# Other filler tiles: the streamed and held operands of the split matmuls start at other bytes of a 256-byte line

## The chip, the core and the metric

One NeuronCore of one Trainium2 chip runs the whole program in one launch. The metric is device time in microseconds (us), the median of several runs. The engines are named as in the profile: PE (TensorE, matmul) and PEld (its weight load), DVE (VectorE), ACT (ScalarE), POOL (GpSimd), SP (SyncE, which issues the DMAs).

## The reference

Two networks run one after the other on 256 tokens of width 1024, in float32, each of two layers. All heavy work is matrix products `x @ w` with x of 256 rows:

```python
# first block, per layer (sizes: 256 x 1024 in, FFN hidden 2816)
u = rms_norm(h, g_mix_pre)
gq, gk, gv, gg, ra_f, ra_b, aq, ak, av, gate_a, gate_b = split(u @ w_in)
...   # gated linear attention, grouped-query attention with axial rope
mixed = sigmoid(gate_a) * branch_a + sigmoid(gate_b) * branch_b
h = h + rms_norm(mixed @ w_out, g_mix_post)
gate, up = split(rms_norm(h, g_ffn_pre) @ w_ffn_in, 2)
h = h + rms_norm((silu(gate) * up) @ w_ffn_out, g_ffn_post)
h = h + rms_norm(sigmoid(h @ w_ple_gate) * (p_i @ w_ple_proj), g_ple_post)
# second block, per layer
x = x + 0.5 * swiglu_ffn(rms_norm(x, ffn1_norm), ffn1_w_in, ffn1_w_out)
...   # recurrent branch (conv, rg_lru) and forgetting attention, merged
x = x + merged @ w_o
x = x + 0.5 * swiglu_ffn(rms_norm(x, ffn2_norm), ffn2_w_in, ffn2_w_out)
x = x + sigmoid(rms_norm(x, ple_norm) @ ple_w_gate + ple_b_gate) * (p_i @ ple_w_proj)
```

## The kernel before

Every big product is made of three matmuls in the format fp32r: a float32 operand is split into a high part and a low part (`hi`, `lo` for a weight; names that end in `h` and `l` for an activation: `xTh`/`xTl`, `hh`/`hl`, `oh`/`ol`, `yh`/`yl`, `mh`/`ml`, `xrh`/`xrl`, `px`), and high x high, high x low and low x high are added up in PSUM. Weights come in tiles of 512 KB from HBM (`raw`), ACT makes `hi` (L250), DVE makes `lo` (L251).

There are two ways to multiply, and they use the operands the other way round:

- `gemm_fm` (L288 to L290): the weight block of 128 columns is **held** in the array (stationary, loaded by a weight load), the activation of 256 columns is **streamed** through it. All of the input projections by features, both FFN inputs, and all products of the second block but three.
- `gemm_tm` (L315 to L317): the activation block of 128 columns is held, the weight of 512 columns is streamed. In the first block it makes w_aq, w_akv, w_gv, w_gg (held: `xT`), w_out (held: `mh`, `ml`), w_ffn_out (held: `hh`, `hl`), w_ple_gate (held: `xr`) and the small w_ple_proj (held: `px`); in the second block w_v, w_q, w_k (held: `xT`).

In both, matmuls follow each other with a new weight load for each; the load for the next one goes on while this one streams. Beside these, small float32 matmuls serve the attentions and the transposes, and L831 is one more fp32r matmul whose streamed operand (`ra`) and held one (`up`) both lie in the mixer's pool.

SBUF is given out by tile pools, one behind the other: constants, `wraw` (raw weights), `whl` (`hi`, `lo`), `act` (`xT`, `R`), `small`, then the temporaries (`t`, `sq`, `px`, ...) and the pool of the stage (mixer or FFN). A filler is a dead tile at the start of a pool (`Net.phase`): nothing reads or writes it, it only moves what lies behind it in this and the later pools. The fillers decide at which byte of a 256-byte line a tile starts. All the blocks inside a tile start at multiples of 512 bytes from it, so all of them have the start byte of the tile.

The order of the instructions is set by a scheduler when the program is built.

Of the kernel before, what the change touches and what calls it, by code (L numbers as in the profile page):

```python
# [11 lines left out]
F32 = mybir.dt.float32  # L12
# [6 lines left out]
P = 128  # L19
# [20 lines left out]
HOLD_B = 4  # L40
LAG = 3

X_PHASE = 64
POOL_PHASE = 32


class Norm:
# [3 lines left out]
    def __init__(self, net, g, tag="xT"):  # L51
        self.net, self.g = net, g
        self.xs = net.pair(net.act, tag)
        self.r = [None, None]
        self.R = net.act.tile([P, S], F32, tag="R", name=net.name("R"), bufs=2)
        self.ssq = [net.small.tile([P, 2], F32, tag="nssq", name=net.name("nssq")) for _ in range(2)]
# [124 lines left out]
class Net:  # L181
    def __init__(self, ctx, tc, a, raw_bufs=4, w_bufs=5, acc_bufs=3):
        self.tc = tc
        self.nc = tc.nc
        self.a = a
        pool = lambda name, bufs, **kw: ctx.enter_context(tc.tile_pool(name=name, bufs=bufs, **kw))
        psum = bass.MemoryType.PSUM
        self.const = pool("const", 1)
        self.wraw = pool("wraw", raw_bufs)
        self.whl = pool("whl", w_bufs)  # L190
        self.act = pool("act", 1)
        self.small = pool("small", 4)
        self.ps = pool("ps", acc_bufs, space=psum)
        self.pt = pool("pt", 2, space=psum)
        self.pm = pool("pm", 2, space=psum)
        self.pg = pool("pg", 1, space=psum)
        self.n = 0
        self.phase(self.act, X_PHASE)
        self.phase(self.small, X_PHASE)


        self.hold = self.held = None
        self.fetched = []
        nc = self.nc
        self.ident = self.const.tile([P, P], F32, name="ident")
        self.h = self.const.tile([P, 2, D], F32, name="h")
        self.expo = self.const.tile([P, 16], F32, name="expo")
        nc.vector.memset(self.expo, -0.5)
        self.ones = self.const.tile([P, P], F32, name="ones")
        nc.vector.memset(self.ones, 1.0)  # L210

    def phase(self, pool, n):

        pool.tile([P, n // 4], F32, tag="phase", name=self.name("phase"), bufs=1)

    def temporaries(self, ctx, bufs):
        self.tmp = ctx.enter_context(self.tc.tile_pool(name=self.name("tmp"), bufs=1))
# [300 lines left out]
def layer_a(net, i, nrm, following):  # L518
    nc, a, tc = net.nc, net.a, net.tc
    with ExitStack() as mx:  # L520
        nrm, px = mixer_a(net, i, mx, nrm)
    with tc.tile_pool(name=net.name("ffn"), bufs=1) as fp:
        net.phase(fp, POOL_PHASE)
        g_post = net.gain(a["g_ffn_post"][i])
        e = ple_proj(net, px, a["w_ple_proj"][i])
        raw = Raw(net, fp)
        net.ffn(nrm, a["w_ffn_in"][i], a["w_ffn_out"][i], net.post_norm(g_post, raw, fp, HOLD_FFN), fp)
        g_post = net.gain(a["g_ple_post"][i])
        nrm = following()
        px = ple_input(net, a["pT_2"][0]) if i + 1 == DEPTH else None  # L530

        def gated(tt, hf, acc):
            cs = slice(hf * 512, (hf + 1) * 512)
            t = net.t()
            nc.scalar.activation(t, acc, AF.Sigmoid)
            nc.vector.tensor_tensor(t, t, e[:, tt, cs], ALU.mult)
            return t

        net.gemm_tm(raw.xs, a["w_ple_gate"][i], net.post_norm(g_post, nrm, fp, HOLD_PLE if i + 1 < DEPTH else HOLD_LAST, gated), lag=LAG)
    return nrm, px  # L540


def ple_input(net, pT):
    with net.urgent(SPLIT_PRIO, 200):
        raw = net.t()
        net.nc.sync.dma_start(out=raw, in_=pT)
        px = (net.t((P, 2, S), F32R, "px"), net.t((P, 2, S), F32R, "px"))
        net.split_fm(raw, *px, 0)
    return px


def ple_proj(net, px, w):
    nc = net.nc
    e = net.t((P, 2, D), tag="e")
    net.gemm_tm(px, w, lambda tt, hf, acc: nc.scalar.copy(e[:, tt, hf * 512:(hf + 1) * 512], acc))
    return e
# [347 lines left out]
def layer_b(net, i, nrm, px, hT, following):  # L904
# [12 lines left out]
    with ExitStack() as cx:  # L917
        ms = mixer_b(net, i, cx, after)
        px = ple_input(net, a["pT_2"][i])
        nrm = NormT(net, hT, col(2))  # L920
        net.gemm_fm(ms, a["w_o"][i], net.add_scaled(hT, 1.0, nrm.blocks), tail=True)
# [20 lines left out]
def mixer_b(net, i, cx, nrm):  # L942
    nc, a, tc = net.nc, net.a, net.tc
    p1 = cx.enter_context(tc.tile_pool(name=net.name("mx"), bufs=1))
    net.phase(p1, POOL_PHASE)
    big = lambda tag, dt=F32: p1.tile([P, KB, S], dt, tag=tag, name=net.name(tag))
    fl = lambda t: t.rearrange("p a b -> p (a b)")
    xs, rs = nrm.xs, nrm.r
# [143 lines left out]
def _build(tc, a, out):  # L1092
    with ExitStack() as ctx:
        net = Net(ctx, tc, a)
        nc = tc.nc
        with ExitStack() as part:
            net.temporaries(part, T_BUFS_A)
            net.split = SPLIT_A
            nrm = lambda pool: first_norm(net, pool)
            nxt = [lambda: Norm(net, net.gain(a["g_mix_pre"][1])), lambda: Norm(net, net.gain(a["ffn1_norm_2"][0]))]  # L1100
            for i in range(DEPTH):
                nrm, px = layer_a(net, i, nrm, nxt[i])

        hp = ctx.enter_context(tc.tile_pool(name="hT", bufs=1))
        net.hp = hp
        net.temporaries(ctx, T_BUFS_B)
        net.split = SPLIT_B
        hT = hp.tile([P, KB, S], F32, name="hT")
        for tt in range(2):
            for hf in range(2):  # L1110
                ps = net.pt.tile([P, 4, P], F32, tag="pt", name=net.name("pt"))
                for j in range(4):
                    kb = hf * 4 + j
                    nc.tensor.transpose(ps[:, j], net.h[:, tt, kb * P:(kb + 1) * P], net.ident)
                nc.scalar.copy(hT[:, hf * 4:hf * 4 + 4, tt * P:(tt + 1) * P], ps)
        gc = hp.tile([P, 16], F32, name="gc")
        nc.sync.dma_start(out=gc, in_=a["gains_last"])
        nxt = [lambda: NormT(net, hT, gc[:, 0:8]), lambda: NormT(net, hT, gc[:, 8:16], out)]
        for i in range(DEPTH):
            nrm, px = layer_b(net, i, nrm, px, hT, nxt[i])  # L1120
# [140 lines left out]
```

## Time and profile before

| | us |
|---|---|
| median of 3 runs (2343.48 to 2346.03) | 2344.41 |
| the profiled execution | 2343.55 |
| its span, first to last instruction | 2341.8 |

The profile is of one execution; its own time is its span and 1.75 us around it. In a timeline the columns are: start in us, duration in us, engine, line, operation, tile written<-tiles read, size, and count. The durations of matmuls overlap (each is printed until its last result is out), so the pace of PE is read from the starts: the time from one start to the next is called a step here.

### The profile page before, as it was taken

Reading aid. Unit: us, or ns where it says so; the run is one execution under the profiler, and the core shown is the slowest. Engines: PE = TensorE matmul, PEld = TensorE weight load, DVE = VectorE, ACT = ScalarE, POOL = GpSimd, SP = SyncE. Lnnn points to the kernel's source line nnn. Section 1 sums busy time; section 2 is a strip of 40 time slices with the busy share of each in tenths; the row PEclk is TensorE's granted clock in tenths of the full one; section 3 lists DMA queues with packets and bytes.
Section 4 is the critical chain, followed back from the end, with each engine's and each line's share of the span. In section 5 each row is a group of like instructions: output and inputs, shape, how many; then the busy total and the mean of one; then the engine's idle time right before and its main releaser. Section 6 shows DMA issues by size and latency. Waiting matters only on the chain.

```text
span 2341.8 us, 42188 instructions
## 1 busy us (share of the span) xinstructions
PE 2291.4 (98%) x16892; PEld 2168.4 (93%) x16892; DVE 1600.6 (68%) x2133; ACT 1335.3 (57%) x2105; POOL 440.3 (19%) x443
## 2 busy tenths in 40 slices
PE   7999999998999999999999999999999999999997
PEld 6899899777899998799999899999999998999997
DVE  7876766477867765766586867665765677766655
ACT  6875554467764644554457765444644457755444
POOL 5222211064302110211001302110111103112101
PEclk9999999999999999999999999999999999999999
DMA  7445566554455666555665545666566655556662
GB/s 250 147 153 160 179 203 186 178 164 148 145 162 173 204 189 185 171 168 187 187 183 184 158 150 185 185 193 187 174 188 184 187 186 166 152 168 191 189 184 96
DMA packets 117102, 411.53 MB, mean 176 GB/s; under 512 B 14114, under 2 KB 16546, under 8 KB 116906
## 3 DMA queue, kind: packets, MB, share of 16 engines
q1 hardware_dynamic: 116906, 408.84, 56.2%
q8 instruction: 133, 2.18, 0.4%
q14 instruction: 63, 0.52, 0.1%
HBM read 407.74 MB, written 1.05 MB: 175 GB/s over the span
## 4 chain that ended last, share of the span: by engine, by line
PE 89%; DVE 4%; POOL 2%; issue 2%; ACT 1%; DMA 1%; SPq 0%; DVEq 0%; POOLq 0%; ACTq 0%
PE acc L290 22%; PE acc L289 22%; PE acc L288 22%; PE acc L315 6%; PE acc L316 6%; PE acc L317 6%; DVE lo L251 2%; PE sc L582 1%; PE po L593 1%; PE gs L890 1%; ACT hi L250 1%; POOL t L713 1%; POOL tab L689 0%; PE sc L606 0%; POOL hg L75 0%
## 5 line engine op out<-in xcount | busy, mean ns | idle before, releaser
L251 DVE TENSOR_TENSOR lo<-raw,hi 128x512 fp32r<-128x512 f32 (+1 forms) x1062 | 983.2, 952 | 439.5 <-ACT hi L250 437.4
L250 ACT ACTIVATE hi<-raw 128x512 fp32r<-128x512 f32 (+1 forms) x1062 | 824.3, 808 | 761.4 <-PE acc L289 396.1
L288 PE MATMUL acc<-xTh,hi 128*128 128x256 f32 x3296 | 924.3, 281 | 10.3 <-ACT t L1060 7.2
L289 PE MATMUL acc<-xTl,hi 128*128 128x256 f32 x3296 | 927.3, 282 | 0.7 <-DVE xTl L130 0.5
L290 PE MATMUL acc<-xTh,lo 128*128 128x256 f32 x3296 | 926.4, 281 | 0.0
L288 PEld LDWEIGHTS acc<-xTh,hi 128*128 128x128 f32 x3296 | 620.1, 188 | 12.5 <-ACT t L1060 7.7
L289 PEld LDWEIGHTS acc<-xTl,hi 128*128 128x128 f32 x3296 | 622.6, 189 | 2.6 <-DVE xTl L130 1.5
L290 PEld LDWEIGHTS acc<-xTh,lo 128*128 128x128 f32 x3296 | 621.3, 189 | 0.4
L396 POOL TENSOR_TENSOR t<-t,R 128x512 f32<-128x512 f32 x66 | 105.0, 1590 | 612.5 <-ACT t L394 612.5
L290 PE MATMUL acc<-hh,lo 128*128 128x256 f32 x704 | 197.1, 280 | 0.0
L288 PE MATMUL acc<-hh,hi 128*128 128x256 f32 x704 | 196.4, 279 | 0.0
L289 PE MATMUL acc<-hl,hi 128*128 128x256 f32 x704 | 196.4, 279 | 0.0
L315 PE MATMUL acc<-hi,xTh 128*128 128x512 f32 x416 | 165.7, 404 | 5.9 <-ACT hi L250 5.9
L316 PE MATMUL acc<-lo,xTh 128*128 128x512 f32 x416 | 167.4, 402 | 2.1 <-DVE lo L251 2.0
L317 PE MATMUL acc<-hi,xTl 128*128 128x512 f32 x416 | 166.4, 401 | 0.1
L289 PEld LDWEIGHTS acc<-hl,hi 128*128 128x128 f32 x704 | 132.4, 188 | 0.0
L290 PEld LDWEIGHTS acc<-hh,lo 128*128 128x128 f32 x704 | 132.1, 188 | 0.0
L288 PEld LDWEIGHTS acc<-hh,hi 128*128 128x128 f32 x704 | 131.6, 187 | 0.0
L315 PEld LDWEIGHTS acc<-hi,xTh 128*128 128x128 f32 x416 | 78.9, 190 | 23.4 <-ACT hi L250 6.0
L316 PEld LDWEIGHTS acc<-lo,xTh 128*128 128x128 f32 x416 | 79.1, 190 | 21.0 <-DVE lo L251 3.8
L317 PEld LDWEIGHTS acc<-hi,xTl 128*128 128x128 f32 x416 | 78.9, 190 | 18.7 <-DVE xTl L351 0.8
L379 DVE TENSOR_TENSOR t<-acc,R 128x512 f32<-128x512 f32 (+1 forms) x84 | 56.8, 676 | 44.1 <-PE acc L290 44.1
(321 smaller groups left out, 3236.5 us busy)
## 6 DMA issues: line engine op xcount, KB each, us to landing
raw<-ffn_w_in SPq DMA_DIRECT2D x176, 512.0 KB, 3.7
raw<-w_ffn_in SPq DMA_DIRECT2D x88, 512.0 KB, 4.3
raw<-ffn_w_out SPq DMA_DIRECT2D x88, 512.0 KB, 3.6
raw<-w_ffn_out SPq DMA_DIRECT2D x44, 512.0 KB, 4.1
raw<-w_gate SPq DMA_DIRECT2D x32, 512.0 KB, 3.6
raw<-w_gab SPq DMA_DIRECT2D x32, 512.0 KB, 3.7
raw<-w_gqk SPq DMA_DIRECT2D x16, 512.0 KB, 4.0
raw<-w_gv SPq DMA_DIRECT2D x16, 512.0 KB, 3.2
```

Source lines behind the costliest of these rows:

```text
L250: nc.scalar.activation(hi[:, cs], raw[:, cs], AF.Copy)
L251: nc.vector.tensor_tensor(lo[:, cs], raw[:, cs], hi.bitcast(F32)[:, cs], ALU.subtract)
L288: nc.tensor.matmul(o, lhsT=hi[:, cs], rhs=xh[:, kb], start=kb == 0, stop=False)
L289: nc.tensor.matmul(o, lhsT=hi[:, cs], rhs=xl[:, kb], start=False, stop=False)
L290: nc.tensor.matmul(o, lhsT=lo[:, cs], rhs=xh[:, kb], start=False, stop=kb == nkb - 1)
L315: nc.tensor.matmul(o, lhsT=xh[:, kb, ts], rhs=hi[:, cs], start=kb == 0, stop=False)
L316: nc.tensor.matmul(o, lhsT=xh[:, kb, ts], rhs=lo[:, cs], start=False, stop=False)
L317: nc.tensor.matmul(o, lhsT=xl[:, kb, ts], rhs=hi[:, cs], start=False, stop=kb == 2 * n - 1)
L379: self.nc.vector.tensor_tensor(v(out), v(acc), r, ALU.mult)
L396: nc.gpsimd.tensor_tensor(tb, tb, nrm.R.unsqueeze(1).to_broadcast([P, 2, S]), ALU.mult)
L582: nc.tensor.matmul(sc[:, j], lhsT=q_t[:, hp * 2 + j, tt * P:(tt + 1) * P], rhs=k_t[:, hp // 2], start=True, stop=True)
L593: nc.tensor.matmul(out[:, j], lhsT=v(jt, hp // 2), rhs=p_t[:, jt], start=jt == 0, stop=jt == 1)
```

## The change

The fillers get other sizes, and the pools of the first block's FFN and of the second block's mixer get different ones. Nothing else is changed. The built programs have the same instructions in the same order on every engine, with the same waits (16,610 on PE, 2,135 on DVE, 1,987 on ACT, 448 on POOL, 812 on SP); only SBUF addresses differ.

```diff
-X_PHASE = 64
-POOL_PHASE = 32
+ACT_PHASE = 192
+SMALL_PHASE = 64
+FFN_A_PHASE = 96
+MIX_B_PHASE = 32
...
-        self.phase(self.act, X_PHASE)
-        self.phase(self.small, X_PHASE)
+        self.phase(self.act, ACT_PHASE)
+        self.phase(self.small, SMALL_PHASE)
...
     def phase(self, pool, n):
-        pool.tile([P, n // 4], F32, tag="phase", name=self.name("phase"), bufs=1)
+        if n:
+            pool.tile([P, n // 4], F32, tag="phase", name=self.name("phase"), bufs=1)
...
 def layer_a(net, i, nrm, following):
...
-        net.phase(fp, POOL_PHASE)
+        net.phase(fp, FFN_A_PHASE)
...
 def mixer_b(net, i, cx, nrm):
...
-    net.phase(p1, POOL_PHASE)
+    net.phase(p1, MIX_B_PHASE)
```

Start bytes within a 256-byte line, read from the addresses of the two built programs:

| tiles | before | after |
|---|---|---|
| `raw`, `hi`, `lo` (weights), constants | 192 (constants 128, 192) | the same |
| `xTh`, `xTl`, `R` | 0 | 128 |
| `oh`, `ol`, `yh`, `yl`, `mh`, `ml`, other big tiles of both mixers, `up`, `ra` | 0 | 128 |
| `hh`, `hl` of the first block, `xrh`, `xrl`, `yg`, and `hg`, `xg` of its FFN stage | 0 | 192 |
| `hh`, `hl` of the second block | 0 | 128 |
| temporaries of the first block (`t`, `sq`, `px`, `e`, `g`) | 224 | 96 |
| temporaries of the second block (`t`, `sq`, `px`) | 0 | 128 |

## Rows read from the trace of the kernel before

**Rows 1.** Chain of work that ended last, shares of the span by line.

```profile
by line: PE acc L290 22.3%; PE acc L289 22.2%; PE acc L288 22.1%; PE acc L315 5.5%; PE acc L316 5.5%; PE acc L317 5.5%; issue 1.6%; DVE lo L251 1.5%; PE sc L582 0.6%; PE po L593 0.6%; PE gs L890 0.6%; ACT hi L250 0.6%; POOL t L713 0.5%; POO
```

**Rows 2.** Page, part 2: the granted TensorE clock in 40 slices, tenths.

```profile
PEclk9999999999999999999999999999999999999999
```

**Rows 3.** Whole span as one window, instructions of L288, then of L315, with counts.

```profile
0.00:2341.80 2341.80, 1271.86 (x4544) 853.21 (x4544) 0.99 0.57 176
...
0.00:2341.80 2341.80, 287.96 (x736) 138.95 (x736) 0.99 0.57 176
```

**Rows 4.** Waits of PE, longest in total: us, times, longest.

```profile
PE acc L288 <- ACT t L1060: 7.2, 2, 3.6
PE ptq L720 <- DVE t L717: 6.9, 4, 2.9
```

**Rows 5.** Timeline of PE: first and last of the 528 matmuls of one ffn1_w_out.

```profile
1577.87 0.28 PE L288 MATMUL acc<-hh,hi 128*128 128x256 f32 x1
...
1639.94 0.28 PE L290 MATMUL acc<-hh,lo 128*128 128x256 f32 x1
```

**Rows 6.** Timeline of PE: first and last of the 264 matmuls of one w_ffn_out.

```profile
406.00 0.40 PE L315 MATMUL acc<-hi,hh 128*128 128x512 f32 x1
...
467.36 0.40 PE L317 MATMUL acc<-hi,hl 128*128 128x512 f32 x1
```

**Rows 7.** Timeline of PE: first and last of the 24 matmuls of two ple_w_proj_2 halves.

```profile
988.20 0.28 PE L288 MATMUL acc<-px,hi 128*128 128x256 f32 x1
...
990.89 0.28 PE L290 MATMUL acc<-px,lo 128*128 128x256 f32 x1
...
2113.72 0.28 PE L288 MATMUL acc<-px,hi 128*128 128x256 f32 x1
...
2116.43 0.28 PE L290 MATMUL acc<-px,lo 128*128 128x256 f32 x1
```

**Rows 8.** Timeline of PE in one w_rnn_out: ends of two stretches between attention's transposes.

```profile
1386.13 0.28 PE L288 MATMUL acc<-yh,hi 128*128 128x256 f32 x1
...
1388.40 0.28 PE L290 MATMUL acc<-yh,lo 128*128 128x256 f32 x1
...
1389.07 0.28 PE L289 MATMUL acc<-yl,hi 128*128 128x256 f32 x1
...
1390.96 0.28 PE L290 MATMUL acc<-yh,lo 128*128 128x256 f32 x1
```

**Rows 9.** Window over the first of these stretches: PE, with its instruction count.

```profile
1386.13:1388.39 2.26, 2.26 (x22) 1.00 0.49 123
```

**Rows 10.** Timeline of PE around two pairs of L831.

```profile
68.74 0.40 PE L831 MATMUL z<-ra,up 98*128 98x256 f32 x2
68.98 0.28 PE L288 MATMUL acc<-xTh,hi 128*128 128x256 f32 x1
...
563.33 0.41 PE L831 MATMUL z<-ra,up 98*128 98x256 f32 x2
563.58 0.28 PE L288 MATMUL acc<-xTh,hi 128*128 128x256 f32 x1
```

**Rows 11.** Lines by form in windows 280:405, then 1453:1577: count, busy us, mean ns.

```profile
L379 DVE TENSOR_TENSOR t<-acc,R 128x512 f32<-128x512 f32 x11 | 7.6, 689 | 8.5 <-PE acc L290 8.5
L399 DVE TENSOR_TENSOR t<-t,acc 128x512 f32<-128x512 f32 x10 | 6.9, 686 | 8.8 <-PE acc L290 8.8
L394 ACT ACTIVATE t<-t 128x512 f32<-128x512 f32 x11 | 6.8, 619 | 0.4 <-DVE t L379 0.4
...
L379 DVE TENSOR_TENSOR t<-acc,R 128x512 f32<-128x512 f32 x11 | 7.6, 691 | 5.8 <-PE acc L290 5.8
L399 DVE TENSOR_TENSOR t<-t,acc 128x512 f32<-128x512 f32 x10 | 6.9, 687 | 6.1 <-PE acc L290 6.1
L394 ACT ACTIVATE t<-t 128x512 f32<-128x512 f32 x11 | 6.8, 617 | 0.2 <-DVE t L379 0.2
```

## Prediction

> **What bounds the kernel now.** I read the chain of waits first. Three lines of `gemm_fm` hold 66.6% of the span (22.1, 22.2 and 22.3%) and three of `gemm_tm` 16.5% [rows 1]: five sixths of the time that counts is the pace at which PE starts its split matmuls. The reader is to see that no other line has more than 1.6%. The clock is no part of it: in every slice it is granted at nine tenths or more of the upper level, 2.4 GHz [rows 2]. PE's waits are short, the longest in total 7.2 us [rows 4]. So a change of that pace goes to the end almost whole, and little else can.
>
> There are 4544 matmuls on each of L288, L289, L290 and 736 on each of L315 to L317 [rows 3]: 13,632 of 256 columns and 2208 of 512. Their pace is the next thing to read, from starts in the timeline. The 528 matmuls of one ffn1_w_out go from 1577.87 to 1639.94: 62.07 us over 527 steps, **117.8 ns** a step [rows 5]. The 264 of one w_ffn_out take 61.36 us over 263 steps, **233.3 ns** [rows 6]. At 2.4 GHz, 256 columns are 106.7 ns and 512 are 213.3 ns, so each step carries 11.1 or 20.0 ns that are not columns. What share of the span lies on the chain gives the steps that count: 0.666 x 2341.8 / 0.1178 = 13,240 of the short ones and 0.165 x 2341.8 / 0.2333 = 1656 (three quarters) of the long ones.
>
> **The change part by part.** No instruction is added, removed or moved; there is no new wait, DMA or queue entry. Three kinds of cost are possible.
>
> *DVE, ACT and POOL on moved tiles: nothing.* The first block's temporaries now start at byte 224, the second's at 0, and the same operations on them take the same time in both: L379 689 and 691 ns, L399 686 and 687, L394 619 and 617 [rows 11]. So start bytes of 96 and 128 should cost these engines nothing; if they did, PE's steps would hide it, as DVE waits for PE here. The raw weights, the target of nearly all DMA bytes, don't move.
>
> *The short steps.* Does PE's step hang on start bytes at all? The trace has one pair to compare. Two halves of ple_w_proj_2 are alike but for `px`, which is still the first block's tile (byte 224) in the one at 988 us and the second block's (byte 0) in the one at 2113 us: 2.69 against 2.71 us over 23 steps, 117.0 against 117.8 ns [rows 7]. That is small and near the rounding of the timeline (two starts of 10 ns each over 23 steps, some 0.4 ns), but it points to yes. A second sign is stronger: in one product with unchanged addresses the pace has two values. From 1386.13 to 1388.40 there are 20 steps (the window counts 22 matmuls, of which two had begun before it [rows 9]), 113.5 ns each; after the next transposes, from 1389.07 to 1390.96, there are 16 steps of 118.1 ns [rows 8]. [...]
>
> What I take as the measure is the distance from the held operand's start byte to the streamed one's, modulo 256. In `gemm_fm` it was 0 - 192 = 64 and becomes 128 - 192 = 192. `gemm_tm` had 192 before (192 - 0), and its 233.3 ns are 116.7 ns for 256 columns. If equal distance gives equal pace, the short step falls from 117.8 to 116.7, by 1.1 ns: 13,240 x 1.1 = **-14.6 us**. The bounds from rows: 113.5 ns, 4.3 ns less (-57 us), and above, the pairs of L831, whose two operands both start at byte 0: 0.24 us for two steps, 120 ns, and 0.25 us, 125 ns, just behind a fast stretch [rows 10]. Taking 120 as the steady one of the two, the upper bound is 2.2 ns more (+29 us). I choose 116.7 since it lies between them and is the pace that most steps at that distance have.
>
> *The long steps.* `gemm_tm` with held `xT` or `mh` goes to distance 192 - 128 = 64, which was that of the short steps: 1.1 ns more for 256 columns, 2.2 for 512. These are 65% of the 1656 steps, 1080: **+2.4 us**. With held `hh` or `xr` both operands start at 192, distance 0, priced by the better pair of L831 at most 120 - 116.7 = 3.3 ns for 256 columns, 6.6 for 512; at least nothing. I take half, 3.3 ns x 540 = **+1.8 us** (0 to +3.6). The few steps of `px` go to distances not seen and are left at nothing.
>
> The sum is -14.6 + 2.4 + 1.8 = **-10.4 us**. The profiled execution took 2343.55 us, 0.86 us under the median, so it becomes 2333.1 and the median **2334 us**, 0.4% less.
>
> **A rule against this.** The rows give the one pair of paces 117.0 and 117.8 for two start bytes [rows 7]. The Trainium skill, page "SBUF — State Buffer", section "Who interferes with whom", says that TensorE has two independent read ports, one for the streamed operand and one for weight loads, and that "PE and ACT never wait on anyone". By that rule start bytes would change nothing and the time would stay 2344 us. The trace does not quite agree: two paces at the same addresses [rows 8] are hard to have without some waiting on a read. It is rival 2.
>
> **Rivals.**
>
> 1. *The fast pace becomes the usual one.* The 113.5 ns hold for a whole stretch once entered and end only when transposes come between [rows 8], so it is a steady state of the same instructions. If the new distance leads into it, 13,240 x 4.3 = -57 us, with the long steps' +4.2: **2291 us**; if the long steps gain in proportion (8.5 ns x 1656 = -14 us), 2273. For it: it exists. Against it: even in this product the pace fell back to 118.1 at unchanged addresses, so it needs more than a start byte.
>
> 2. *Nothing happens.* All new start bytes are multiples of 32 and for streamed operands a half line away from the old ones; the difference of byte 224 could be one of odd 32-byte steps only. Then **2344 us**. For it: `gemm_tm` with 264 steps at 233.3 and `gemm_fm` at 117.8 differ by only 1% per column though their distances differ by 128. Against it: they do differ.
>
> 3. *The new distance is worse for the short steps.* The mechanism is the one in which the weight load and the stream meet on the same line, as in L831 with equal start bytes; the new distance is 64 bytes on the other side of that point. At 120 ns the short steps cost +29 us: **2373 us**, plus the long steps' up to +6. It decides from 118.2 ns on (0.35 ns x 13,240 = 4.7 us, 0.2%). For it: 120 to 125 ns occur [rows 10]. Against it: `gemm_tm` runs at this distance without such a pace.
>
> **How the numbers follow.** A measurement of this kernel can tell about 0.2% (4.7 us) from no change. My forecast of a slightly better step has 0.30, rival 1 0.22, rival 2 0.22, rival 3 0.26. Faster by over 0.2% is the forecast and rival 1, 0.52; within 0.2% is rival 2, 0.22; slower is rival 3, 0.26. The likeliest single case is the forecast, with its own range of 2326 to 2340. As cases of both signs hold most of the chance, the range has to reach from inside rival 1 to inside rival 3: 2282 to 2372 leaves out the far half of rival 1's span and rival 3 above 120 ns, about 2 in 10.
>
> **What would show it.** The first and last start of the same ffn1_w_out in the new trace: 61.5 us over 527 steps if the forecast is right, 59.8 for rival 1, 62.07 for rival 2, over 63 for rival 3. For the long steps, one w_ffn_out (held `hh`) at 61.4 to 63.1 us over 263 steps, and w_out and w_v at 235.5 ns. DVE's L379 and L399 should stay at 0.69 us; if they grow, the part on the other engines is wrong. The forecast fails if the pace hangs on each start byte by itself and not on the distance, or if the new pace has two values as now and mixes them by stage.

## The result, and the profile after

| us | before | after |
|---|---|---|
| median (lowest to highest), 4 executions each | 2344.25 (2343.48 to 2346.03) | 2317.82 (2315.75 to 2322.82) |
| the profiled execution | 2343.55 | 2315.75 |
| its span | 2341.8 | 2313.9 |

The ratio is 0.9889, with a 95% interval of 0.9871 to 0.9908: the change saves 1.1%, 26 us, where 0.4% had been forecast. The new kernel's four times spread over 7 us, the old one's over 2.5; in the later runs the old one's spread over 4 to 9, in 9 to 18 executions each. Every line from `Net.phase` on has moved in the file: L288 to L290 (`gemm_fm`) are now L292 to L294, L315 to L317 (`gemm_tm`) are L319 to L321, and L379, L394, L399 are L383, L398, L403.

The chain of waits, shares of the span by line, answers to [rows 1]:

```profile
by line: PE acc L292 22.2%; PE acc L293 22.1%; PE acc L294 22.1%; PE acc L319 5.3%; PE acc L320 5.3%; PE acc L321 5.2%; issue 1.7%; DVE lo L255 1.5%; ACT hi L254 0.8%; PE sc L586 0.6%; PE po L597 0.6%; PE gs L894 0.6%; POOL t L717 0.5%; PE 
```

The granted clock in part 2 of the page, as [rows 2], and the longest waits of PE (us in total, times, longest), as [rows 4]:

```profile
PEclk9999999999999999999999999999999999999999
```

```profile
PE acc L292 <- ACT t L1064: 8.5, 2, 4.3
PE acc L319 <- ACT hi L254: 6.2, 1, 6.2
PE ptq L724 <- DVE t L721: 5.8, 3, 2.7
```

The same six lines hold five sixths of a shorter span, the clock is as it was, and no wait has come or gone that would pay for 26 us. So the steps themselves are shorter. The product that the prediction had named as its witness [rows 5] is called ffn1_w_out there; by the order of the program it is layer 0's ffn2_w_out (the next weights to come are those of ple_w_gate). It runs as it did before; its first and last start in the timeline of PE:

```profile
1552.16 0.28 PE L292 MATMUL acc<-hh,hi 128*128 128x256 f32 x1
...
1614.23 0.28 PE L294 MATMUL acc<-hh,lo 128*128 128x256 f32 x1
```

62.07 us over 527 steps, 117.8 ns; the first ffn1_w_out, from 1106.88 to 1168.95 us, takes the same. The input product of the first block's FFN, whose streamed `xT` starts at the same byte 128, does not. Below is the window over all of it but its first matmuls (length, PE busy, count of matmuls, clock, DMA share, GB/s), and then first and last start of the 216 matmuls of w_f and w_rgate behind w_v, in layer 0 and in layer 1:

```profile
278.26:397.62 119.36, 119.36 (x1055) 1.00 0.67 203
```

```profile
1214.09 0.28 PE L292 MATMUL acc<-xTh,hi 128*128 128x256 f32 x1
...
1238.48 0.28 PE L294 MATMUL acc<-xTh,lo 128*128 128x256 f32 x1
...
1874.92 0.28 PE L292 MATMUL acc<-xTh,hi 128*128 128x256 f32 x1
...
1900.24 0.28 PE L294 MATMUL acc<-xTh,lo 128*128 128x256 f32 x1
```

The window counts 1055 matmuls, one of which had begun before it: 1053 steps in 119.36 us, **113.3 ns**. The 216 matmuls take 24.39 us in layer 0 and 25.32 us in layer 1: 113.4 and 117.8 ns over 215 steps, with the same operations on tiles at the same start bytes. These are the two paces that the trace of before had shown side by side in w_rnn_out [rows 8]. What is new is how often the shorter one holds. I counted it from the starts of the whole trace: of the steps of L288 to L290 before, 181 lay between 112 and 115 ns and 13,244 between 116 and 121; of those of L292 to L294 now, 4852 and 8566. That is 1.3% before and **36%** after, with means of 113.3 and 117.8 ns.

The long steps are shorter too: first and last start of a w_ffn_out (264 matmuls, held `hh` at byte 192), of a w_out (96, held `mh` at 128) and of a w_v (96, held `xT` at 128):

```profile
397.73 0.39 PE L319 MATMUL acc<-hi,hh 128*128 128x512 f32 x1
...
457.36 0.39 PE L321 MATMUL acc<-hi,hl 128*128 128x512 f32 x1
...
246.22 0.39 PE L319 MATMUL acc<-hi,mh 128*128 128x512 f32 x1
...
267.97 0.40 PE L321 MATMUL acc<-hi,ml 128*128 128x512 f32 x1
...
1192.11 0.39 PE L319 MATMUL acc<-hi,xTh 128*128 128x512 f32 x1
...
1213.85 0.39 PE L321 MATMUL acc<-hi,xTl 128*128 128x512 f32 x1
```

59.63 us over 263 steps is 226.7 ns, where it was 233.3 [rows 6]; 21.75 and 21.74 us over 95 are 228.9 and 228.8.

The sum over the trace says where the time came from. The short steps (112 to 121 ns) add up to 1558.8 us in 13,418 of them, before to 1580.4 in 13,425: **-21.6 us**. The long ones (224 to 237 ns) add up to 482.6 us in 2110, before to 493.0 in 2113: **-10.4 us**. All the rest of PE's time is 3.8 us more. Together -28.2, against 27.9 us between the two spans.

### The profile page after: what moved, and what is told of

It is laid out like the page before. It is cut to its first block, busy times and chain, and to the rows that moved or that the text cites. A ratio compares the mean times of both kernels' runs of the same rounds, so it can differ in the third digit from the quotient of the medians.

```text
span 2313.9 us, 42188 instructions
## 1 busy us (share of the span) xinstructions
PE 2262.1 (98%) x16892; PEld 2147.9 (93%) x16892; DVE 1602.1 (69%) x2133; ACT 1333.4 (58%) x2105; POOL 442.6 (19%) x443
## 4 chain that ended last, share of the span: by engine, by line
PE 88%; DVE 4%; POOL 2%; ACT 2%; issue 2%; DMA 1%; SPq 0%; DVEq 0%; POOLq 0%; ACTq 0%
PE acc L292 22%; PE acc L293 22%; PE acc L294 22%; PE acc L319 5%; PE acc L320 5%; PE acc L321 5%; DVE lo L255 1%; ACT hi L254 1%; PE sc L586 1%; PE po L597 1%; PE gs L894 1%; POOL t L717 1%; PE sc L610 0%; POOL hg L78 0%; POOL tab L693 0%
## 5 line engine op out<-in xcount | busy, mean ns | idle before, releaser
L292 PE MATMUL acc<-xTh,hi 128*128 128x256 f32 x3296 | 923.5, 281 | 11.1 <-ACT t L1064 8.5
L294 PE MATMUL acc<-xTh,lo 128*128 128x256 f32 x3296 | 923.5, 280 | 0.0
L292 PEld LDWEIGHTS acc<-xTh,hi 128*128 128x128 f32 x3296 | 621.8, 189 | 13.3 <-ACT t L1064 8.9
L294 PEld LDWEIGHTS acc<-xTh,lo 128*128 128x128 f32 x3296 | 627.0, 190 | 0.4
L292 PE MATMUL acc<-hh,hi 128*128 128x256 f32 x704 | 197.8, 281 | 0.0
L294 PE MATMUL acc<-hh,lo 128*128 128x256 f32 x704 | 197.8, 281 | 0.0
L319 PE MATMUL acc<-hi,xTh 128*128 128x512 f32 x416 | 164.6, 401 | 6.4 <-ACT hi L254 6.2
L321 PE MATMUL acc<-hi,xTl 128*128 128x512 f32 x416 | 165.4, 399 | 0.8 <-DVE xTl L355 0.8
L294 PEld LDWEIGHTS acc<-hh,lo 128*128 128x128 f32 x704 | 134.4, 191 | 0.0
L292 PEld LDWEIGHTS acc<-hh,hi 128*128 128x128 f32 x704 | 132.1, 188 | 0.0
L319 PEld LDWEIGHTS acc<-hi,xTh 128*128 128x128 f32 x416 | 79.1, 191 | 22.7 <-ACT hi L254 6.1
L321 PEld LDWEIGHTS acc<-hi,xTl 128*128 128x128 f32 x416 | 79.2, 190 | 17.8 <-DVE xTl L355 1.5
L383 DVE TENSOR_TENSOR t<-acc,R 128x512 f32<-128x512 f32 (+1 forms) x84 | 56.8, 676 | 41.1 <-PE acc L294 41.1
```

The costliest lines, as they stand in the source:

```text
L292: nc.tensor.matmul(o, lhsT=hi[:, cs], rhs=xh[:, kb], start=kb == 0, stop=False)
L294: nc.tensor.matmul(o, lhsT=lo[:, cs], rhs=xh[:, kb], start=False, stop=kb == nkb - 1)
L319: nc.tensor.matmul(o, lhsT=xh[:, kb, ts], rhs=hi[:, cs], start=kb == 0, stop=False)
L321: nc.tensor.matmul(o, lhsT=xl[:, kb, ts], rhs=hi[:, cs], start=False, stop=kb == 2 * n - 1)
L383: self.nc.vector.tensor_tensor(v(out), v(acc), r, ALU.mult)
```

## Experiments

**Theory A**: the short step has two steady paces, 113.3 and 117.8 ns; which one a stretch runs at is settled when the stream is taken up again after an interruption (transposes, or a product of the other kind) and holds until the next one; the start bytes only change how often the shorter one is met. **Theory B**: each pair of start bytes has a pace of its own. **Theory C**: what runs beside PE sets it (the moved temporaries, DVE and ACT). The paces below are each worked out as above, from the first and the last start of a stretch.

**One part of the change alone: `xT` and `R` moved, all else where it was.**

```diff
-SMALL_PHASE = 64
-FFN_A_PHASE = 96
+SMALL_PHASE = 192
+FFN_A_PHASE = 32
```

> Only xT (and R) starts at byte 128; every other tile is back at its byte of before. Theory A (two steady paces of 113.3 and 117.8 ns, the same in both kernels; the start bytes decide how often an interruption of the stream is followed by the fast one): products with xT are fast after about half of the interruptions, in the first block above all as in the changed kernel; the products with oh, yh, mh and hh streamed from byte 0 go back to 117.8 in all but a few places; w_ffn_out (held hh at 0) goes back to 233.3. Time about 2322 to 2332 us. Theory B (each pair of start bytes has one pace of its own): products with xT have one pace throughout, 115 to 116 ns, in both blocks. Theory C (the moved temporaries of the other engines make the difference): they are at their bytes of before here, so all steps are 117.8 and the time is 2344 us.

2331.74 us (2319.21 to 2335.36), ratio 0.9945 [0.9925, 0.9966]. Both paces are there, 12% of the short steps at 113.3 ns in the profiled execution, while w_ffn_out stays at 233.3 ns.

**The other part: everything moved but `xT` and `R`.**

```diff
-ACT_PHASE = 192
-SMALL_PHASE = 64
+ACT_PHASE = 64
+SMALL_PHASE = 192
```

> The other half: xT and R back at byte 0, everything else as in the changed kernel (hh and xr of the first block at 192, hh of the second block, oh, yh, mh at 128, temporaries at 96 and 128). Theory A: products with xT are at 117.8 ns in all but a few places, those with oh and yh keep their fast stretches (after some of the interruptions), w_ffn_out stays at 226.7 ns for 512 columns; time about 2334 to 2339 us. Theory B: the same sign, one pace for each tile. Theory C: most of the gain stays, about 2320 us, with xT products fast in the first block.

2335.39 us (2326.39 to 2335.95), ratio 0.9957 [0.9942, 0.9973]. 7.5% of the short steps run at 113.3 ns, one whole ffn1_w_out among them; the other three FFN output products of the second block run at 117.8. w_ffn_out takes 226.8 ns a step, w_v (held `xT` back at 0) 233.4. So each part brings some, and neither a fixed pace for the short step. Here tiles of two start bytes follow each other in one stream, and the pace can change at the border, with no other instruction between: first and last start of that ffn1_w_out (layer 1's),

```profile
1787.12 0.28 PE L292 MATMUL acc<-hh,hi 128*128 128x256 f32 x1
...
1846.86 0.28 PE L294 MATMUL acc<-hh,lo 128*128 128x256 f32 x1
```

59.74 us over 527 steps, 113.4 ns, from byte 128, while the `xT` ahead of it and behind it, from byte 0, run at 117.8. An interruption, as theory A has it, is thus not the only way in.

**The first block's `hh` and `xr` held at 128 in place of 192.**

```diff
-FFN_A_PHASE = 96
+FFN_A_PHASE = 32
```

> The changed kernel with only the first block's FFN pool moved: hh and xr held at byte 128 instead of 192 (streamed weights stay at 192). If the held byte decides the long step, w_ffn_out goes from 226.7 to the mixed 229 to 230 ns of w_out, whose mh is held at 128, and the time is 1 to 3 us longer (2319 to 2322 us). If the long step is the same for 128 and 192, w_ffn_out stays at 226.7 and the time is 2316 to 2319 us. Theories A, B and C do not differ on it.

2316.17 us (2312.67 to 2331.56), ratio 0.99 [0.9859, 0.994]. As a whole it can't be told from the change, but its w_ffn_out can:

```profile
397.60 0.39 PE L319 MATMUL acc<-hi,hh 128*128 128x512 f32 x1
...
457.80 0.40 PE L321 MATMUL acc<-hi,hl 128*128 128x512 f32 x1
```

60.20 us over 263 steps, 228.9 ns, the value of the other tiles held at 128.

**An interruption put in on purpose.** One to four float32 matmuls of one column, that go nowhere, in front of the third block of each second-block FFN input (layer 0's ffn1 and ffn2: 1 and 2; layer 1's: 3 and 4). Addresses stay as in the change.

```diff
+    def poke(self, hi, n):
+        ps = self.pg.tile([P, n], F32, tag="pg", name=self.name("poke"))
+        for k in range(n):
+            self.nc.tensor.matmul(ps[:, k:k + 1], lhsT=hi.bitcast(F32)[:, 0:P], rhs=self.ones[:, 0:1], start=True, stop=True)
...
+                if poke and u == 16:
+                    self.poke(hi, poke)
```

> The changed kernel with 1, 2, 3 and 4 extra float32 matmuls of one column (results not used) in front of the third 128-column block of the four FFN input products of the second block, where the changed kernel runs at 117.8 ns for 1524 to 1570 steps on end each time. Nothing else moves. Theory A: each of these pokes is a new interruption after which the fast pace can be entered, about half of the time; a stretch that becomes fast stays so to the end of the FFN output product, 1480 steps x 4.4 ns = 6.5 us less for each, against some 0.2 to 0.6 us for the poke: with two of four, about 2306 us. Theory B and theory C: the stretches have the same operands, start bytes and neighbours as before, so they stay at 117.8 ns behind the poke and the time grows by about 1 us to 2318 us.

**2305.62 us** (2298.06 to 2309.26), ratio 0.9835 [0.9814, 0.9856]: with added work it beats the change, of which no execution here or below took less than 2311. The timeline at the second poke (its two matmuls are four records on one row), and then the first and last start of that FFN's output product:

```profile
1449.55 0.28 PE L302 MATMUL acc<-xTl,hi 128*128 128x256 f32 x1
1449.67 0.28 PE L303 MATMUL acc<-xTh,lo 128*128 128x256 f32 x1
1449.79 0.28 PE L301 MATMUL acc<-xTh,hi 128*128 128x256 f32 x1
1449.90 0.50 PE L281 MATMUL poke<-ones,hi 128*128 128x1 f32 x4
1450.27 0.36 PE L302 MATMUL acc<-xTl,hi 128*128 128x256 f32 x1
1450.47 0.28 PE L303 MATMUL acc<-xTh,lo 128*128 128x256 f32 x1
1450.58 0.28 PE L301 MATMUL acc<-xTh,hi 128*128 128x256 f32 x1
1450.70 0.28 PE L302 MATMUL acc<-xTl,hi 128*128 128x256 f32 x1
...
1561.42 0.28 PE L301 MATMUL acc<-hh,hi 128*128 128x256 f32 x1
...
1621.15 0.28 PE L303 MATMUL acc<-hh,lo 128*128 128x256 f32 x1
```

Ahead of the poke the steps are 0.12 us, behind it 0.11 to 0.12, and 111 us later they are still 59.73 us over 527, 113.3 ns, in the very product that takes 62.07 us in the changed kernel (1552.16 to 1614.23 above). Tiles, weights and neighbours are the same on both sides of the poke: theory C is out, and so is B for this pair of bytes. The fourth poke changed the pace in the same way. Ahead of the first and the third the stream was at 113.3 ns already and stayed there: the third to the end of its FFN, the first up to transposes at 1002 us, behind which the pace was 117.8 for 1553 matmuls. So two of the four stretches owe their pace to a poke. That the time forecast, about 2306 us, was met so closely is in part luck: in this profile the first block's two FFN inputs, which no poke touches, run at 117.8 ns, and layer 1's ffn1 had its 113.3 without one.

**Single pokes at eight places**: the same float32 matmul, once each, in all six FFN inputs and both second-block w_attn_out, in the changed kernel and in the kernel before.

```diff
+                if poke and u == poke:
+                    self.poke(hi)
...
+    net.gemm_fm(xb, wb, epi, poke=poke)
```

> The changed kernel with one extra one-column float32 matmul (result not used) in each of the six FFN input products (in front of the third block; in the second block's first FFN in front of the seventh, behind the last interruption that undid an earlier one) and one in each w_attn_out of the second block. Theory A with entry by the poke: behind each poke the pace is 113.3 ns to the next interruption; fast share of the 256-column steps from 36% to over 75%, time 2285 to 2300 us. If the pokes of the earlier run were fast by chance, about half of the eight stretches are fast: 2300 to 2315 us.

> The kernel before, with its start bytes, and the same eight pokes. If the entry alone decides (the start bytes only shift how entries fall), the pokes make the long stretches fast here too: about 9000 steps x 4.4 ns = 40 us less, 2300 to 2310 us, and the fillers would not be needed. If the start bytes decide into which pace this poke leads, the stretches stay at 117.8 ns: 2343 to 2346 us, the eight pokes costing some 2 us. Between the two for a chance of its own at each poke.

In the changed kernel 2310.47 us (2303.64 to 2312.05), ratio 0.986 [0.9843, 0.9877]; in the kernel before 2336.4 us (2331.62 to 2343.13), ratio 0.9977 [0.9962, 0.9992]. In each of the two profiles the pace is 113.3 ns behind three of the eight pokes and 117.8 behind five; in the changed kernel one of the three has 113.3 ahead of it too. The shorter pace is thus to be had at the old start bytes as well, where it is rare otherwise (1.3% of the short steps, with the pokes 13%). One poke is no sure way into it.

**Other start bytes**, with `hh` and `xr` of the first block held at 192 throughout. Each run sets two fillers; that of byte 64 reads

```diff
-ACT_PHASE = 192
-FFN_A_PHASE = 96
+ACT_PHASE = 128
+FFN_A_PHASE = 160
```

> The changed kernel with all streamed tiles (and the held xT, mh) at byte 64, hh and xr of the first block held at 192 as in the changed kernel. Theory A: steps of 256 columns still come in the paces 113.3 and 117.8, in some other shares, so the time lies between 2286 us (all fast) and 2345 us (all slow). Theory B: one new pace of its own. The long steps with held xT and mh show the held byte 64; with hh they stay at 226.7. No forecast of the share is made: the two known bytes 0 and 128 gave 1% and 36%.

> All streamed tiles and all held activations at byte 192, the byte of the weights (distance 0). Held at 192, all long steps should be at 226.7 ns (xT and mh too, from 228.9): 1.5 us less on the chain than in the changed kernel. For the 256-column steps theory A: the same two paces in some other share, 2284 to 2345 us. My forecast's rival of a collision at equal bytes: one pace above 118.2 ns, over 2345 us.

> All streamed tiles and xT, mh at byte 96, first block's hh, xr at 192 as in the changed kernel. Theory A (two steady paces, 113.3 and 117.8 ns, at streamed bytes 0 and 128, and one pace elsewhere, 118.7 at 64 and 120.0 at 192): one pace between those of 64 and 128, 115 to 119 ns, about 2330 to 2355 us; w_ffn_out 226.7 ns, w_out and w_v between 232.3 and 228.9 ns. If the two paces are general, stretches at 113.3 and at 117.8 appear here too and the time is 2300 to 2330 us.

> All streamed tiles and xT, mh at byte 160. Theory A: one pace between the 117.8 of 128 and the 120.0 of 192, about 2345 to 2360 us; w_out and w_v between 228.9 and 226.7 ns. If the two paces are general, stretches at 113.3 and 117.8 and 2300 to 2330 us.

> All streamed tiles and xT, mh at byte 224, where one short stretch of the kernel before ran at 117.0 ns. One pace of 117.0 ns over long stretches: 13,240 steps at 0.8 ns less than before, -11 us, and the long steps' -7 us with w_ffn_out at 226.7 ns: about 2326 us. If the two paces are general, 113.3 and 117.8 mixed and 2300 to 2330 us. Held xT and mh at 224 weren't seen: 226.7 to 233.3 ns.

First and last start of the first ffn1_w_out (528 matmuls), streamed at 64, at 192 and at 224; then those of the 216 matmuls behind w_v in both layers, streamed at 96:

```profile
1128.10 0.28 PE L292 MATMUL acc<-hh,hi 128*128 128x256 f32 x1
...
1190.63 0.28 PE L294 MATMUL acc<-hh,lo 128*128 128x256 f32 x1
```

```profile
1130.15 0.28 PE L292 MATMUL acc<-hh,hi 128*128 128x256 f32 x1
...
1193.39 0.28 PE L294 MATMUL acc<-hh,lo 128*128 128x256 f32 x1
```

```profile
1119.51 0.28 PE L292 MATMUL acc<-hh,hi 128*128 128x256 f32 x1
...
1180.99 0.28 PE L294 MATMUL acc<-hh,lo 128*128 128x256 f32 x1
```

```profile
1233.17 0.28 PE L292 MATMUL acc<-xTh,hi 128*128 128x256 f32 x1
...
1258.68 0.28 PE L294 MATMUL acc<-xTh,lo 128*128 128x256 f32 x1
...
1897.27 0.28 PE L292 MATMUL acc<-xTh,hi 128*128 128x256 f32 x1
...
1922.50 0.28 PE L294 MATMUL acc<-xTh,lo 128*128 128x256 f32 x1
```

With the weights held at 192, and the steady paces found in stretches of over a hundred matmuls (short step), and in w_out (long step, held `mh` at the same byte as the streamed tiles). Each ratio is to executions of the kernel before beside that run; their medians were 2342.19 us for 64 and 192 and 2341.95 for 96, 160 and 224:

| streamed byte | short step, ns | long step, ns | median, us | ratio |
|---|---|---|---|---|
| 0 (before) | 117.8, seldom 113.3 | 233.3 | 2344.25 | 1 |
| 64 | 118.7, seldom 120.0 | 232.3 | 2350.89 | 1.0038 [1.0023, 1.0053] |
| 96 | 117.3 and 118.7 | 233.3 | 2338.71 | 0.9989 [0.998, 0.9999] |
| 128 (after) | 113.3 and 117.8 | 228.9 | 2317.82 | 0.9889 [0.9871, 0.9908] |
| 160 | 118.3 | 233.3 | 2345.63 | 1.0019 [1.001, 1.0029] |
| 192 | 120.0 | 227.0 | 2360.98 | 1.0083 [1.0066, 1.01] |
| 224 | 116.7, seldom 117.8 | 233.3 | 2326.09 | 0.994 [0.9921, 0.996] |

Theory A as it was forecast, 113.3 and 117.8 ns everywhere in other shares, missed at 64 and at 192. Two paces are seen at five of the seven bytes, but not the same two everywhere: at 96 they are 117.3 and 118.7 ns, and the two layers differ as in the changed kernel; at 64 one stretch of 216 matmuls takes 120.0 ns a step, at 224 two of 114 and 139 take 117.8, and all their other long ones the usual pace. Only at 160 and 192 is there one pace alone, as theory B has it. At 224, where [rows 7] gave the 117.0 ns, 2326 us was expected and 2326.09 came. The long step follows the held byte: 233.3 at 0, 96, 160 and 224, 232.3 at 64, 228.9 at 128, 226.7 to 227.0 at 192. w_ffn_out, held at 192 in all five runs, takes 226.7 to 226.9. The forecasts that w_out and w_v at 96 and 160 would lie between their neighbours missed; that equal bytes, 192 and 192, give the short step one pace above 118.2 ns and a time over 2345 us came true.

**What decides an entry? Three pokes at each of the eight places.**

```diff
-        ps = self.pg.tile([P, 1], F32, tag="pg", name=self.name("poke"))
-        self.nc.tensor.matmul(ps, lhsT=hi.bitcast(F32)[:, 0:P], rhs=self.ones[:, 0:1], start=True, stop=True)
+        ps = self.pg.tile([P, 3], F32, tag="pg", name=self.name("poke"))
+        for k in range(3):
+            self.nc.tensor.matmul(ps[:, k:k + 1], lhsT=hi.bitcast(F32)[:, 0:P], rhs=self.ones[:, 0:1], start=True, stop=True)
```

> The changed kernel with three one-column float32 matmuls, instead of one, in front of one block of each of six FFN-in products and both second-block w_attn_out. If it is the number of interruptions that leads into 113.3 ns (counts of 1 to 4 all did in the first poke run, single ones 3 times of 8 in the second), at least seven of the eight stretches run at 113.3 ns and the time is under 2300 us (fast share over 75%: 13,400 x 0.39 x 4.45 = 23 us under the changed kernel's 2318). If an entry is chance at about two in five, three or so are fast and the time is 2303 to 2315 us, with other ones fast than before.

2320.84 us (2314.77 to 2324.62), ratio 0.9896 [0.9879, 0.9913]: the time of the change without any poke. Two of eight are at 113.3 ns behind the poke. Three in a row do no better than one.

**Odd or even?** Two runs with other numbers of pokes at the eight places, odd where the other is even, and the changed kernel itself in a second profile.

```diff
-    net.gemm_fm(xb, wb, epi, poke=poke)
+    net.gemm_fm(xb, wb, epi, poke=poke, n=2)
...
-after.blocks), fp, fm=True, poke=16 if i else 48)
+after.blocks), fp, fm=True, poke=16 if i else 48, n=(2, 1)[i])
```

> The changed kernel with float32 matmuls of one column in front of one block of each of eight products: one at the two first-block FFN inputs and at layer 1's ffn1, two at layer 0's ffn1, both ffn2 and both w_attn_out. In the poke runs so far, ffn2 was entered fast after 2 and 4 and slow after 1 and 3; layer 1's ffn1 fast after 1 and 3; layer 0's ffn1 and w_attn_out slow after 1 and 3. If the number's parity at a place decides, all eight are fast here and the time is under 2300 us. If it is chance, three or so are fast and the time is 2303 to 2320 us.

> As the run before it, with the counts' parity turned: two at the first-block FFN inputs and at layer 1's ffn1, three at layer 0's ffn1, both ffn2 and both w_attn_out. If parity at a place decides, all eight are slow and the time is 2330 to 2338 us. If it is chance, three or so are fast and the time is 2303 to 2320 us.

> The changed kernel as it is, for a second profile of it: if an entry's pace is fixed by the program, its stretches have the same paces as in the first profile and the time is 2316 us; if it is partly chance in each execution, some long stretches have the other pace.

| place (layer 0, layer 1): ahead-behind (matmuls) | single | three | counts a | counts b |
|---|---|---|---|---|
| first-block FFN input | 118-113, 113-113 (1) | 113-113, 118-118 (3) | 118-113, 113-113 (1) | 113-118, 118-113 (2) |
| second-block ffn1 | 118-118, 118-113 (1) | 118-118, 118-113 (3) | 113-118 (2), 118-113 (1) | 118-113 (3), 118-113 (2) |
| w_attn_out | 118-118, 118-118 (1) | 118-118, 118-118 (3) | 118-113, 118-113 (2) | 118-118, 118-118 (3) |
| second-block ffn2 | 118-118, 118-118 (1) | 118-118, 118-118 (3) | 113-118, 113-118 (2) | 118-118, 118-118 (3) |

The table gives the pace ahead of each poke and behind it in the changed kernel's four runs with pokes at eight places, in whole ns, and the number of matmuls. (Ahead of w_attn_out's there are but seven steps.) The times are 2307.74 us (2298.38 to 2311.6), ratio 0.985 [0.9831, 0.987], for a, and 2317.38 (2310.57 to 2323.72), ratio 0.9902 [0.9883, 0.992], for b. Parity as it was forecast, that it decides the pace at a place, falls: ffn2 comes out at 117.8 after one, two and three, though it had come out at 113.3 after two and four in the first poke run. But the forecasts didn't ask for the pace ahead of the poke, and with it the number tells more. In the changed kernel's five poke runs an even number changed the pace at all ten places that had one, from 117.8 to 113.3 at six and from 113.3 to 117.8 at four. An odd number left 113.3 as it was at all five such places, and led from 117.8 to 113.3 at six of 21. This was read from the traces afterwards; no run was made to test it. Layer 0's ffn1 in counts a, from the second matmul of its stretch to the two pokes and behind them:

```profile
994.40 0.28 PE L300 MATMUL acc<-xTh,hi 128*128 128x256 f32 x1
...
1004.15 0.28 PE L302 MATMUL acc<-xTh,lo 128*128 128x256 f32 x1
...
1004.83 0.28 PE L301 MATMUL acc<-xTl,hi 128*128 128x256 f32 x1
...
1178.67 0.28 PE L300 MATMUL acc<-xTh,hi 128*128 128x256 f32 x1
```

9.75 us over 86 steps is 113.4 ns, 173.84 us over 1476 is 117.8: this poke led out of the shorter pace.

There is chance in it as well, as the second profile of the changed kernel shows: the same FFN input as above, and layer 1's ffn1_w_out,

```profile
278.23 0.28 PE L294 MATMUL acc<-xTh,lo 128*128 128x256 f32 x1
...
402.25 0.28 PE L294 MATMUL acc<-xTh,lo 128*128 128x256 f32 x1
...
1768.35 0.28 PE L292 MATMUL acc<-hh,hi 128*128 128x256 f32 x1
...
1828.08 0.28 PE L294 MATMUL acc<-hh,lo 128*128 128x256 f32 x1
```

The first took 119.36 us over 1053 steps in the first profile and takes 124.02 here, 117.8 ns; the second took 62.07 (1767.41 to 1829.48) and takes 59.73, 113.3 ns. The program, its addresses and all its waits are the same; 41% of the short steps are at 113.3 ns here. The chip may be another one than in the first profile, but the four executions of this run, all on one chip, spread as well: the median is 2316.74 us (2311.21 to 2323.07), and the spread is of the size of two or three such stretches: 1053 x 4.45 ns is 4.7 us.

## Why the prediction was right in sign and wrong in size

**What bounds the kernel: right.** The six lines keep their share of the chain, and a shorter pace went to the end almost whole: -32.0 us of steps, 3.8 given back, 27.9 of span.

**DVE and ACT at no cost: right.** The lines by form in windows 273:397 and 1428:1552 answer to [rows 11]; the temporaries now start at 96 and at 128:

```profile
L383 DVE TENSOR_TENSOR t<-acc,R 128x512 f32<-128x512 f32 x11 | 7.6, 690 | 7.4 <-PE acc L294 7.4
L398 ACT ACTIVATE t<-t 128x512 f32<-128x512 f32 x11 | 6.8, 618 | 0.8 <-DVE t L383 0.8
...
L383 DVE TENSOR_TENSOR t<-acc,R 128x512 f32<-128x512 f32 x11 | 7.6, 691 | 5.8 <-PE acc L294 5.8
L403 DVE TENSOR_TENSOR t<-t,acc 128x512 f32<-128x512 f32 x10 | 6.9, 688 | 6.1 <-PE acc L294 6.1
```

**The short steps: the step that failed is "If equal distance gives equal pace".** The distance of 192 had 116.7 ns in `gemm_tm`; in `gemm_fm` it has 113.3 and 117.8, as the distance of 64 had before. The term was -14.6 us and came to -21.6 (4671 more steps at the shorter pace, 4.44 ns each, are 20.7 of it). Its size was near by luck: no long stretch of the changed kernel runs at 116.7 ns, which is the pace at streamed byte 224. There the pair in [rows 7] had pointed the right way, 117.0 against 117.8; the runs give 116.7 over 527 steps. But it was a sign about byte 224 and not about 128. The second sign, the two paces of [rows 8], stood at unchanged addresses: it was no sign that start bytes matter, but it held the pace that came, 113.5 ns, which the prediction kept as a bound.

**The long steps: wrong in sign, and the larger part of the miss.** +4.2 us was forecast, 235.5 ns for w_out and w_v and 61.4 to 63.1 us for w_ffn_out; -10.4 us came, with 228.9 ns and 59.6 us. It is the same failed step. Equal start bytes were priced as the worst case, after L831; for the long step they are the best that was seen (226.7 ns, both at 192), while for the short step they are the worst (120.0). The two terms of +2.4 and +1.8 had each the wrong sign.

**Rivals.** Rival 1 named the mechanism: 113.5 ns as "a steady state of the same instructions", entered and left at transposes [rows 8]. What spoke against it, that "it needs more than a start byte", was right too, and the truth lay between: 36% of the steps, where it had all or none, for a start byte changes how often an entry leads there. Rival 2, no change, rested on a half line being neutral: at byte 128 the two paces are indeed those of byte 0, yet the share of each isn't. Rival 3's 120 ns exists, at equal bytes, on all four ffn1 and ffn2 output products streamed at 192; 64 bytes off on the far side of that point, at 128, it doesn't.

**The rule.** Start bytes alone, with the same instructions, move the time from 2318 to 2361 us and the long step from 226.7 to 233.3 ns. The Trainium skill, page "SBUF — State Buffer", section "Who interferes with whom", says that TensorE's two read ports are independent and that "PE and ACT never wait on anyone". What the prediction drew from it, that start bytes would change nothing, these runs contradict; whether a wait on a read is the cause they don't show.

**What would show it.** The product of [rows 5] at 62.07 us answered, taken by itself, for rival 2. One stretch was a poor witness where the pace has two values "and mixes them by stage", which the prediction had named as a way to fail.

**What stays open.** Why a stream settles at one of two paces at most bytes no run settled. Nor did one settle what in an entry picks the pace: an even number of interrupting matmuls changed it each time in the changed kernel, but behind an odd number, and behind the program's own interruptions, either pace came. That the weight load and the stream hinder each other inside the reads of PE, on which rival 3 rests, no trace shows. Weights at other bytes than 192 weren't tried.

## What to carry to other kernels

Where back-to-back matmuls bound a kernel, read the pace of each long stretch from first start, last start and count, and compare like stretches of several layers and executions: a pace of two values hides in a mean. Start bytes of held and streamed tiles are worth a few runs, for here they moved the whole time by 1.9%, but the best pair for one shape is the worst for another, so each shape wants its own measurement. If a shape has two paces, one or more matmuls of one column put into a long stretch can move it to the shorter one, but also out of it; the gain is partly chance, so it needs several executions to be judged (the first poke run, 2305.62 us, and counts a, 2307.74, are the best measured here, and their ranges overlap).

## What was not expected of the hardware

- A stream of split matmuls at unchanged addresses keeps one of two paces, 113.3 or 117.8 ns for 256 columns, over up to 1546 matmuls in a row at the first and 1570 at the second, and the same program takes the other one in another execution.
- The step of 512 columns, weights streamed at 192, is 6.6 ns shorter with the held activation at byte 192 too than at 0. Even this isn't quite fixed: in the first profile of the changed kernel 40 matmuls held at 128, from 507.13 to 516.23 us, run at 233.3 ns a step, and in the second one w_v, held at 128, took 22.17 us over 95 steps, 233.4 ns, as if held at 0:

```profile
1851.88 0.40 PE L319 MATMUL acc<-hi,xTh 128*128 128x512 f32 x1
...
1874.05 0.39 PE L321 MATMUL acc<-hi,xTl 128*128 128x512 f32 x1
```

- Two float32 matmuls of one column in front of a stretch of 1545 cost 0.4 us on the spot (0.68 us from 1449.79 to 1450.47, for two steps that would take 0.24) and saved 6.9 us behind it (1545 x 4.45 ns), where they led into the shorter pace.
